# Two-trunk encoder: neighbourhood-attention probabilities of six heads turned by VectorE and DRAM instead of TensorE

## The chip, the core and the metric

The kernel runs on one core of a Trainium2 chip. The metric is device time in microseconds (us), the median of several runs of the whole program. The core has a matmul engine (TensorE, PE in the profile, with its weight loads as PEld), VectorE (DVE), ScalarE (ACT), GpSimd (POOL), and SyncE (SP), which here only issues transfers. Each engine works through its own instructions in order, and waits on semaphores for the others. Transfers go through queues of SP, ACT and GpSimd to 16 DMA engines that all share. Matmul results land in PSUM; everything else lives in SBUF.

## The reference

Two inputs, a prompt of 1024 tokens and a sample of 512, go through one encoder layer of width 1024, all in fp32:

```python
xn = rmsnorm(x);  z = xn @ w_in          # q,k,v of A; q,k,v of B; gate A; gate B
o_a = grouped-query attention(qa, ka, va)           # branch A, 8 heads of 64
o_b = neighbourhood attention(qb, kb, vb, rpb)      # branch B, 8 heads of 64
x = x + (sigmoid(ga) * (o_a @ w_proj_a) + sigmoid(gb) * (o_b @ w_proj_b)) @ w_out
x = x + relu(rmsnorm(x) @ w_mlp_up) ** 2 @ w_mlp_down;  y = rmsnorm(x)
```

In branch B the tokens form a grid 64 wide. A query sees a window of 8 rows by 16 columns around it; a learned bias per head is added to each score, everything outside the window is masked, and softmax and the product with the values follow.

## The kernel before

The short trunk (512 tokens, names with `s0`) runs first, then the long one (1024 tokens, `NB = 2`, names with `s1`), then both MLPs. A product of fp32 matrices is three reduced-precision matmuls, high·high, high·low and low·high (`mm3`, lines 195 to 197). So every operand is kept as a high part, which ScalarE makes by a copy that rounds (`ACTIVATE`), and a low part, which VectorE makes by subtracting (`TENSOR_TENSOR`).

The change is in branch B of the long trunk, 797 to 1067 us of the profiled span. Its work is 32 units: 8 heads, and for each four strips of 16 grid columns (j = 1, 2, 0, 3). A strip has 256 queries in two halves of 128, and each half sees 12 rows of 32 columns, 384 keys. One unit is three steps, each a function:

- `s_unit`: two score matmuls 128x384 a half (`sbs`, line 971: the queries hold both parts, the keys come as high and as low part) into one of two PSUM buffers; GpSimd adds bias and mask (`bms`, 957); VectorE's custom reduction adds them to the scores, negates and takes the minimum (974); ScalarE's Exp with its sum (`pbs`, 979); VectorE's reciprocal (981); GpSimd's scaling (982).
- `t_unit`: the probabilities have queries on the partitions, but the value product needs keys there. TensorE transposes six 128x128 pieces (`ptbs`, 994) into PSUM; ScalarE copies the high part, VectorE subtracts the low part (`bhs`, 999 and 1000).
- `v_unit`: four matmuls with the values as the stationary operand (`obs`, 1013). Keys that both halves share are one matmul of 512 columns (2 parts x 2 halves x 128 queries), the others one of 256. `finish_o` adds the two partition halves (`ot_Bs`, `os_Bs`, 439 to 452) and stores the result to DRAM (`obds`, 453) by ACT's queue.

A unit's transposes are written one unit behind its scores and its value product one more (`LS = LV = 1`). Between the steps a filler (`Fill.pull`) puts pieces of other work: 129 steps of the gate projection, three matmuls each (`gpss`), whose tanh is stored by ACT's queue (`zgs`, 430). Every eighth unit brings the query and key projection of the next two heads (`pqbs`, `pkbs`, 96 matmuls); over the last eight units the filler is the output projection of branch A (`proj_a`, `ppas`). The tile scheduler sets the final order on each engine: it may move an instruction against the program's text unless it is marked by `keep_in_program_order`, and nothing on TensorE is marked here. It also inserts the semaphores.

SP's queue loads weights (`raw_..`), bias rectangles (`rects`) and the values in the strips' layout (`vss`, 878; 16 transfers a head). GpSimd's queue carries only the mask and eight key copies here.

## Time and profile before

| | |
|---|---|
| median of 3 runs | 2143.84 us (2143.38 to 2143.88) |
| the profiled execution | 2144.47 us |
| its span in the trace | 2142.7 us |
| granted TensorE clock | 0.999 |
| TensorE, VectorE, ScalarE, GpSimd busy | 99%, 68%, 53%, 17% of the span |
| DMA, mean | 165 GB/s |
| long branch B | 797 to 1067 us: TensorE busy 268.4 of 270.0 us |

The trace's names leave out buffer numbers: `sbs1_0_1` in the program is `sbs` there. In the program, `sbs1_2_1` is the long trunk's head 2, strip 1. A timeline row gives start, length, engine, line and operation, the tile written and the tiles read, and how many instructions of a kind follow each other; in square brackets stands the idle time ahead and what ended it. A group row gives the instructions of one line and shape with total busy time and mean ns of one. A waits row gives the total, the number and the longest of the waits of one line for another. A row with a queue and a kind gives packets, MB and the share of 16 engines' time; a transfer row the median us from issue to landing. `SPq`, `ACTq` and `POOLq` are the issues on a queue.

### The profile page before, as it was taken

What the parts mean: (1) busy time and instruction counts of PE and PEld (TensorE: products, weight loads), DVE (VectorE), ACT (ScalarE), POOL (GpSimd) and SP (SyncE); (2) the same over time, 40 slices, a digit from 0 to 9 for tenths busy, and PEclk for the clock granted to TensorE, in tenths of its full rate; (3) what the DMA queues carried; (4) which work ended last, traced back from release to release, by engine and by line L of the source; (5) the groups of instructions that cost most, each with busy time, mean ns of one, the idle gap of its engine ahead of it and who ended that gap; (6) DMA issues with size and microseconds to landing.
All of it is one profiled execution on the core that took longest, in us unless ns stands there. A gap on an engine that the chain in (4) does not pass through costs nothing.

```text
span 2142.7 us, 32089 instructions
## 1 busy us (share of the span) xinstructions
PE 2115.4 (99%) x10967; PEld 1846.9 (86%) x10967; DVE 1462.8 (68%) x2793; ACT 1145.3 (53%) x2511; POOL 356.1 (17%) x446
## 2 busy tenths in 40 slices
PE   9999999999999999999999999999999999999998
PEld 8888778888897888887888899999999988888887
DVE  6665786767657755556882877778777777759563
ACT  6664653767566644555530566566555643434352
POOL 2232310323232223333200200003000000000000
PEclk9999999999999999999999999999999999999999
DMA  6437557520122133433472665578545799688561
GB/s 191 133 99 208 157 162 249 186 71 25 56 78 69 42 95 108 132 117 111 142 234 105 212 198 182 174 243 208 161 145 155 256 353 342 213 275 280 174 201 64
DMA packets 321259, 354.08 MB, mean 165 GB/s; under 512 B 31551, under 2 KB 255431, under 8 KB 321095
## 3 DMA queue, kind: packets, MB, share of 16 engines
q1 hardware_dynamic: 278647, 280.96, 42.0%
q10 hardware_dynamic: 35296, 50.88, 6.8%
q0 software_dynamic: 7152, 20.19, 3.5%
q8 instruction: 87, 1.43, 0.3%
q14 instruction: 77, 0.63, 0.1%
HBM read 264.85 MB, written 87.88 MB: 165 GB/s over the span
## 4 chain that ended last, share of the span: by engine, by line
PE 68%; issue 1%; DVE 1%; DMA 0%; ACT 0%; SPq 0%; POOL 0%; POOLq 0%; ACTq 0%; DVEq 0%
PE dn L196 7%; PE dn L197 7%; PE dn L195 7%; PE ua L195 2%; PE ua L197 2%; PE ua L196 2%; PE ud L195 2%; PE ud L197 2%; PE ud L196 2%; PE uc L195 2%; PE uc L197 2%; PE uc L196 2%; PE gpss L195 2%; PE gpss L197 2%; PE gpss L196 2%; PE ops L197 1%
## 5 line engine op out<-in xcount | busy, mean ns | idle before, releaser
L197 PE MATMUL dn<-wd,al 128*128 128x512 f32 x624 | 242.8, 389 | 0.0
L196 PE MATMUL dn<-wd,ah 128*128 128x512 f32 x624 | 242.8, 389 | 0.0
L195 PE MATMUL dn<-wd,ah 128*128 128x512 f32 x624 | 242.7, 389 | 0.0
L1273 ACT ACTIVATE ah<-ar 128x512 fp32r<-128x512 f32 x168 | 104.2, 627 | 202.6 <-PE dn L196 190.4
L1274 DVE TENSOR_TENSOR al<-ar,ah 128x512 fp32r<-128x512 f32 x168 | 114.0, 686 | 75.3 <-ACT ah L1273 67.2
L195 PEld LDWEIGHTS dn<-wd,ah 128*128 128x128 f32 x624 | 117.2, 188 | 24.5
L197 PEld LDWEIGHTS dn<-wd,al 128*128 128x128 f32 x624 | 117.2, 188 | 24.2
L196 PEld LDWEIGHTS dn<-wd,ah 128*128 128x128 f32 x624 | 117.2, 188 | 24.2
L749 POOL TENSOR_SCALAR ps<-ps,rls 128x1024 f32<-128x1024 f32 (+1 forms) x96 | 96.8, 1009 | 225.7 <-DVE rls L748 200.3
L788 ACT ACTIVATE pths<-pTs 128x512 fp32r<-128x512 f32 x160 | 94.0, 597 | 74.0 <-PE pTs L783 71.8
L789 DVE TENSOR_TENSOR ptls<-pTs,pths 128x512 fp32r<-128x512 f32 x160 | 107.5, 686 | 37.7 <-ACT pths L788 36.7
L743 DVE TENSOR_REDUCE nms<-ss 128x1 f32<-128x1024 f32 (+1 forms) x96 | 99.8, 1040 | 25.6 <-PE ss L741 25.1
L195 PE MATMUL gpss<-xs_0h,w_gs 128*128 128x512 f32 x256 | 105.6, 412 | 0.5 <-DVE ot_Bs L440 0.4
L746 ACT ACTIVATE ps<-ss,nms 128x1024 f32<-128x1024 f32 (+1 forms) x96 | 93.1, 971 | 22.8 <-DVE nms L743 20.1
L783 PEld LDWEIGHTS pTs<-ident,ps 128*128 128x128 f32 x640 | 78.0, 140 | 28.5 <-POOL ps L749 4.3
L180 POOL TENSOR_TENSOR rs_f<-ms_f,mhalf 128x1 f32<-128x1 f32 x6 | 4.0, 667 | 590.7 <-DVE ms_f L176 590.7
L197 PE MATMUL gpss<-xs_0h,w_gs 128*128 128x512 f32 x256 | 101.1, 395 | 0.3 <-DVE w_gs L190 0.3
L196 PE MATMUL gpss<-xs_0l,w_gs 128*128 128x512 f32 x256 | 101.0, 394 | 0.0
L783 PE MATMUL pTs<-ident,ps 128*128 128x128 f32 x640 | 99.0, 274 | 1.3 <-DVE ptls L789 0.6
L1273 ACT ACTIVATE A<-S 128x512 fp32r<-128x512 f32 x128 | 75.9, 623 | 31.2 <-DVE S L1336 22.4
L957 POOL TENSOR_TENSOR bms<-rects,msks 128x384 f32<-128x384 f32 (+1 forms) x72 | 70.1, 976 | 128.7 <-DVE nmbs L974 107.8
L1392 ACT ACTIVATE c<-c 128x384 f32<-128x384 f32 x96 | 50.3, 524 | 69.6 <-DVE c L1391 69.5
(330 smaller groups left out, 6418.7 us busy)
## 6 DMA issues: line engine op xcount, KB each, us to landing
ar<-ud SPq DMA_DIRECT2D x120, 512.0 KB, 5.2
br<-in_w_mlp_down_dram SPq DMA_DIRECT2D x72, 512.0 KB, 5.4
rawu<-in_w_mlp_up_dram SPq DMA_DIRECT2D x64, 512.0 KB, 4.1
ud<-c ACTq DMA_DIRECT2D x128, 192.0 KB, 3.3
raw_gs<-in_w_in_dram SPq DMA_DIRECT2D x32, 512.0 KB, 4.0
zgs<-sgs ACTq DMA_DIRECT2D x48, 256.0 KB, 2.2
ud<-cs SPq DMA_DIRECT2D x64, 192.0 KB
raw_os<-in_w_out_dram SPq DMA_DIRECT2D x16, 512.0 KB, 3.8
```

What stands on the lines that cost most here:

```text
L195: nc.tensor.matmul(out, ah, bh, start=start, stop=False, **kw)
L196: nc.tensor.matmul(out, ah, bl, start=False, stop=False, **kw)
L197: nc.tensor.matmul(out, al, bh, start=False, stop=stop, **kw)
L743: nc.vector.tensor_reduce(nm_, s, axis=AX.X, op=ALU.max, negate=True)
L746: nc.scalar.activation(p, s, AF.Exp, bias=nm_, accum_out=l)
L749: nc.gpsimd.tensor_scalar(p, p, rl, 1.0, op0=ALU.mult, op1=ALU.mult)
L783: nc.tensor.transpose(pt[:, j * P : (j + 1) * P], PP[u, j][:, kc * P : (kc + 1) * P], ident)
L788: nc.scalar.activation(hi, pt, AF.Copy)
L789: nc.vector.tensor_tensor(lo, pt, hi.bitcast(F32), op=ALU.subtract)
L957: nc.gpsimd.tensor_tensor(bm.rearrange("p (r c) -> p r c", c=32), rects[h][:, ir : ir + kr_n, jr : jr + 32], msk[:, hf * 3 + ct, :].rearra ...
L1273: nc.scalar.activation(hi, src, AF.Copy)
L1274: nc.vector.tensor_tensor(lo, src, hi.bitcast(F32), op=ALU.subtract)
```

## The change

It concerns the long trunk's branch B only. For the 24 units of the first six heads (`moved`):

- Both halves' probabilities lie in one tile of 128x768 (two buffers), written by Exp in an order of 32-wide blocks. VectorE transposes each 32x32 block in place, one instruction of 128x768 (`turn`), written between the next unit's two reductions and its Exps. GpSimd's queue stores the tile to DRAM (`tbs`, 393 KB), and four transfers on SP's queue fetch it back with the blocks placed as a whole transpose needs them (`fetch_t`; 32 partitions, four runs of 768 bytes each). ScalarE copies the high part from SBUF, VectorE subtracts the low part in place, both 128x768.
- The split comes three units behind the scores, the value product four. The value product is six matmuls of 256 columns, since the two halves' keys no longer lie side by side.
- The last eight units keep TensorE's transposes, one and two units behind.

For the whole of the long branch B, TensorE's instructions are marked to keep program order (`held_pe`), the four score matmuls of a unit stand ahead of its two reductions, the gate and output stores go by SP's queue (`store[0]`), and the values of heads 1 to 6 are loaded strip by strip instead of head by head. The filler's pulls become 5 or 6 with a mean of 5.33 instead of 5.67, what is left of the gate projection is drained ahead of the 25th unit's split, and `proj_a` begins one unit earlier.

```diff
+    held_pe = []
+    def mul(out, a, b, **kw):
+        op = nc.tensor.matmul(out, a, b, **kw)
+        if held_pe:
+            tc.keep_in_program_order(op)
...
-                    nc.scalar.dma_start(dst[c * P : (c + 1) * P, tb * 512 : tb * 512 + 512], sg)
+                    store[0].dma_start(dst[c * P : (c + 1) * P, tb * 512 : tb * 512 + 512], sg)
...
-            nc.scalar.dma_start(dst, b[:, :n])
+            store[0].dma_start(dst, b[:, :n])
...
+            moved = set(units[: n - 8]) if NB == 2 else set()
...
+                if before is not None:
+                    before()
+                pm = ph.tile([P, halves * nkey], F32, tag="pb", name=f"pb{N}_{h}_{j}", bufs=4 // halves)
+                if u in moved:
+                    pm = pm.rearrange("p (b f k i) -> p b f k i", b=4, f=halves, i=32)
...
+            def turn(u):
+                h, j = u
+                pm = PT[u]
+                blocks = pm.rearrange("p b f k i -> p (b f k) i")
+                tc.keep_in_program_order(nc.vector.transpose(blocks, blocks))
+                PT[u] = dram.tile([P, 4, halves * nkc * 32], F32, name=f"tb{N}_{h}_{j}")
+                nc.gpsimd.dma_start(PT[u], pm.rearrange("p b f k i -> p b (f k i)"))
+
+            def fetch_t(u):
+                h, j = u
+                hl = ph.tile([P, 2, 4, halves, nkc, 32], F32R, tag="bh", name=f"bh{N}_{h}_{j}", bufs=3)
+                turned = PT[u].rearrange("(a i) b w -> b i a w", i=32)
+                for b in range(4):
+                    nc.sync.dma_start(
+                        hl[b * 32 : b * 32 + 32, 1].rearrange("p a f k i -> p a (f k i)").bitcast(F32), turned[b]
+                    )
+                PT[u] = hl
...
+                if u in moved:
+                    hi, lo = (PT[u][:, i].rearrange("p a f k i -> p (a f k i)") for i in range(2))
+                    nc.scalar.activation(hi, lo.bitcast(F32), AF.Copy)
+                    nc.vector.tensor_tensor(lo, lo.bitcast(F32), hi.bitcast(F32), op=ALU.subtract)
+                    return
...
+                if u in moved:
+                    seq = [(k + hf, hf, hf + 1) for hf in range(2) for k in range(nkc)]
...
-            LS, LV = (1, 1) if NB == 2 else (2, 1)
+            if moved:
+                store[0] = nc.sync
+                held_pe.append(1)
+            for i, u in enumerate(units):
+                ls = 3 if u in moved else 3 - NB
+                due_t.setdefault(i + ls, []).append(u)
+                due_v.setdefault(i + ls + 1, []).append(u)
...
-                    f = (5 if i < LS else 2 + i % 2) if NB == 1 else 5 + (i % 3 > 0)
+                    f = (5 if i < 2 else 2 + i % 2) if NB == 1 else 5 + (i % 3 == 0)
...
+                if 0 < i <= n and units[i - 1] in moved:
+                    fetch_t(units[i - 1])
```

Over the program TensorE has 144 transposes fewer, 48 value products of 512 columns fewer and 96 of 256 more. VectorE has 24 block transposes and 24 subtracts from SBUF more and 48 from PSUM fewer; GpSimd's queue has 24 stores more, SP's 96 fetches and the 40 stores that leave ACT's. Three places of the order matter. The first is TensorE at the head of the branch (`pkbs` is the first head pair's key projection, `sbs1_0_1` the first unit's scores); before:

```order
L195 MATMUL pkbs1_0_1_9339<-xs1_1h1_4943,w_bks1_0_9224 128x512
L196 MATMUL pkbs1_0_1_9339<-xs1_1l1_4945,w_bks1_0_9224 128x512
L197 MATMUL pkbs1_0_1_9339<-xs1_1h1_4943,w_bks1_0_9224 128x512
L195 MATMUL gpss1_3328_0_0_9420<-xs1_0h0_4501,w_gs1_3328_0_9230 128x512
L196 MATMUL gpss1_3328_0_0_9420<-xs1_0l0_4503,w_gs1_3328_0_9230 128x512
L197 MATMUL gpss1_3328_0_0_9420<-xs1_0h0_4501,w_gs1_3328_0_9230 128x512
L195 MATMUL gpss1_3328_0_0_9420<-xs1_0h0_4501,w_gs1_3328_0_9230 128x512
L196 MATMUL gpss1_3328_0_0_9420<-xs1_0l0_4503,w_gs1_3328_0_9230 128x512
L197 MATMUL gpss1_3328_0_0_9420<-xs1_0h0_4501,w_gs1_3328_0_9230 128x512
L971 MATMUL sbs1_0_1_9371<-kBs1_0_0_9235,qBs1_0_9234 128x384
L195 MATMUL gpss1_3328_0_0_9420<-xs1_0h0_4501,w_gs1_3328_0_9230 128x512
```

The same place of the change (every matmul now has the line of `mul`, 197):

```order
L197 MATMUL pkbs1_0_1_9339<-xs1_1l1_4945,w_bks1_0_9224 128x512
L197 MATMUL pkbs1_0_1_9339<-xs1_1h1_4943,w_bks1_0_9224 128x512
L197 MATMUL sbs1_0_1_9371<-kBs1_0_0_9235,qBs1_0_9234 128x384 x4
L197 MATMUL gpss1_3328_0_0_9402<-xs1_0h0_4501,w_gs1_3328_0_9230 128x512
L197 MATMUL gpss1_3328_0_0_9402<-xs1_0l0_4503,w_gs1_3328_0_9230 128x512
```

The four scores now come straight behind the key projection, ahead of the first gate matmul. The second place is VectorE in the unit whose scores are `sbs1_2_2` (head 2, its second strip); before:

```order
L440 TENSOR_TENSOR ot_Bs1_1_0_10192<-obs1_1_0_10187,ot_Bs1_1_0_10192 64x512
L974 ISA sbss1_2_2_0_10201,nmbs1_2_2_0_10202<-sbs1_2_2_10198,bms1_2_1_0_10104 128x384
L452 TENSOR_TENSOR os_Bs1_1_0_10195<-ot_Bs1_1_0_10192 64x256
L190 TENSOR_TENSOR w_bqs1_2_10053<-raw_bqs1_2_0_10051,w_bqs1_2_10053 128x512
L974 ISA sbss1_2_2_1_10212,nmbs1_2_2_1_10213<-sbs1_2_2_10198,bms1_2_1_1_10117 128x384
L981 RECIPROCAL rlbs1_2_2_0_10207<-lbs1_2_2_0_10205 128x1
L1000 TENSOR_TENSOR bhs1_2_1_10232<-ptbs1_2_1_0_10230,bhs1_2_1_10232 128x3x128
L1000 TENSOR_TENSOR bhs1_2_1_10232<-ptbs1_2_1_1_10231,bhs1_2_1_10232 128x3x128
L981 RECIPROCAL rlbs1_2_2_1_10218<-lbs1_2_2_1_10216 128x1
```

The same unit of the change:

```order
L1002 ISA sbss1_2_2_0_10112,nmbs1_2_2_0_10113<-sbs1_2_2_10107,bms1_2_1_0_10034 128x384
L460 TENSOR_TENSOR os_Bs1_1_1_10099<-ot_Bs1_1_1_10096 64x256
L1002 ISA sbss1_2_2_1_10115,nmbs1_2_2_1_10116<-sbs1_2_2_10107,bms1_2_1_1_10038 128x384
L1046 STREAM_TRANSPOSE pbs1_2_1_10051<-pbs1_2_1_10051 128x768
L1036 RECIPROCAL rlbs1_2_2_0_10124<-lbs1_2_2_0_10122 128x1
L1036 RECIPROCAL rlbs1_2_2_1_10129<-lbs1_2_2_1_10127 128x1
L1067 TENSOR_TENSOR bhs1_1_0_10028<-bhs1_1_0_10028 128x768
L448 TENSOR_TENSOR ot_Bs1_1_2_10170<-obs1_1_2_10163,ot_Bs1_1_2_10170 64x512
```

The two subtracts of the unit before are gone; the transpose of the unit before stands behind the two reductions, and the subtract is that of a unit three back. The third place is SP's queue a little further on, in the change (`bhs` the fetch, `obds` the output store, `zgs` the gate store, `vss` a value strip):

```order
L438 DMA zgs1_1_4662<-sgs1_3328_3_0_10220 128x512
L461 DMA obds1_4664<-os_Bs1_1_0_10248 64x256
L1056 DMA bhs1_2_2_10251<-tbs1_2_2_10197 32x4x192 x4
L900 DMA vss1_2_10064<-vds1_4660 32x4x128 x4
L438 DMA zgs1_1_4662<-sgs1_3328_3_1_10306 128x512
L461 DMA obds1_4664<-os_Bs1_1_3_10319 64x256
L1056 DMA bhs1_2_0_10322<-tbs1_2_0_10272 32x4x192 x4
```

Before, SP's queue held there only loads of weights, bias rectangles and values:

```order
L223 DMA raw_bqs1_2_0_10051<-in_w_in_dram 128x8x128
L223 DMA raw_bks1_2_0_10054<-in_w_in_dram 128x8x128
L872 DMA rects1_3_10130<-biases_97 128x768
L223 DMA raw_gs1_3328_4_0_10174<-in_w_in_dram 128x8x128
L878 DMA vss1_3_10132<-vds1_4660 32x4x128 x16
```

Each unit now has four fetches and an output store in the line of SP's issues, between the loads.

More of the change, by code (lines that the diff above doesn't have):

```diff
@@ L406, in run @@
         fill = Fill()
+        store = [nc.scalar]
         def gate(goff, dst, c0=0, c1=NC8):
@@ L815, in load_o @@
                 t = slot([P, 2, T], F32R, f"oX{N}_{br}_{k}", first and br + k == 0)
-                cut = partial(split, t[:, 0, :], t[:, 1, :], raw[:, :T])
+                cut = partial(split, t[:, 0, :], t[:, 1, :], raw[:, :T], br == 0 and NB == 2)
                 if hold is None:
@@ L863, in run @@
             rects, strips, bms, PT = {}, {}, {}, {}
+            units = [(h, j) for h in range(8) for j in (1, 2, 0, 3)]
+            n = len(units)
+            moved = set(units[: n - 8]) if NB == 2 else set()
             def raw_here(name):
@@ L970, in s_unit @@
                         ]
-                        nc.tensor.matmul(so, qk[h // 2][0][:, h % 2, q0 : q0 + P], kv, start=(i == 0), stop=(i == 1))
+                        mul(so, qk[h // 2][0][:, h % 2, q0 : q0 + P], kv, start=(i == 0), stop=(i == 1))
+                sums = []
+                for hf in range(halves):
+                    nm = f"{N}_{h}_{j}_{hf}"
                     sb = ph.tile([P, nkey], F32, tag="sb", name=f"sbs{nm}", bufs=2)
@@ L1055, in run @@
                     if i % 8 == 7 and qp is not None:
+                        if NB == 2 and i == n - 9:
+                            for _ in range(NC8):
+                                next(qp)
+                            for _ in range(3):
+                                oa_held.pop(0)()
                         for _ in qp:
```

160 lines of the change are left out of this document (111 added, 49 removed).

## The prediction, made before the change ran

> **What bounds the kernel now.** I read the page's engine totals first, then TensorE's waits in the long branch B (797 to 1067 us), then that stretch cut into windows.
>
> ```profile
> PE 2115.4 (99%) x10967; PEld 1846.9 (86%) x10967; DVE 1462.8 (68%) x2793; ACT 1145.3 (53%) x2511; POOL 356.1 (17%) x446
> PE sbs L971 <- DVE kBs L937: 0.8, 1, 0.8
> PE gpss L195 <- DVE bhs L1000: 0.4, 1, 0.4
> PE obs L1013 <- issue: 0.2, 1, 0.2
> core 0: us, PE busy (x) PEld busy (x) DVE busy (x) ACT busy (x) POOL busy (x), PEclk, DMA share, GB/s
> 830.00:865.00 35.00, 34.82 (x162) 28.27 (x161) 16.65 (x46) 13.50 (x27) 7.38 (x10) 1.00 0.28 80
> 865.00:901.00 36.00, 36.00 (x186) 30.14 (x185) 24.17 (x67) 22.10 (x49) 15.98 (x21) 1.00 0.52 154
> ```
>
> TensorE is busy throughout at the full granted clock; in 270 us of branch B it waits three times, 1.4 us in all. So a matmul taken away there is time taken away, and a new wait there is time added. The two windows show two kinds of stretch. 865 to 901 holds six attention units (6.0 us each): VectorE is 67% busy, DMA 52%. 830 to 865 holds mostly the next pair's query and key projection: both are slack. Three six-unit stretches (18 of the 24 moved units) are where the new work must fit; the two units at each projection have room.
>
> **The transposes removed.** A matmul's busy time overlaps its neighbour's, so I price by starts.
>
> ```profile
> 867.92 0.82 PE L994 MATMUL ptbs<-ident,pbs 128*128 128x128 f32 x6
> 868.81 0.39 PE L196 MATMUL gpss<-xs_0l,w_gs 128*128 128x512 f32 x1
> 869.04 0.39 PE L197 MATMUL gpss<-xs_0h,w_gs 128*128 128x512 f32 x1
> 870.66 0.85 PE L1013 MATMUL obs<-bhs,vss 128*128 128x512 f32 x4
> 871.34 0.52 PE L971 MATMUL sbs<-kBs,qBs 128*128 128x384 f32 x2
> 639.76 0.28 PE L195 MATMUL zvs<-wh_vs,xs_1h 128*128 128x256 f32 x1
> 639.88 0.28 PE L196 MATMUL zvs<-wl_vs,xs_1h 128*128 128x256 f32 x1
> ```
>
> Matmuls of 512 columns start 0.23 apart (868.81, 869.04). Six transposes and one such matmul, whose own row is left out, take 867.92 to 868.81, 0.89 us; the transposes cost 0.89 − 0.23 = 0.66 a unit, 0.11 each. 24 × 0.66 = **−15.8 us**.
>
> **The value product.** It is now six matmuls of 256 columns in place of two of 512 and two of 256. Before it takes 870.66 to 871.34, 0.68 us. Matmuls of 256 columns start 0.12 apart in the value projection, each with its own weight load, so 6 × 0.12 = 0.72: +0.04 × 24 = **+1.0**. That its moving operand comes in runs of 32 columns I price at nothing: the scores' keys already come so (a 32-column window of each grid row). 256 columns at half of 512's 0.23 would make it 0.69, so zero is the other bound.
>
> **The head of the branch.** Program order now puts the first unit's four scores straight behind the last key projection; before, six gate matmuls filled that place.
>
> ```profile
> 795.90 0.39 PE L197 MATMUL pkbs<-xs_1h,w_bks 128*128 128x512 f32 x1
> 797.57 0.45 PE L971 MATMUL sbs<-kBs,qBs 128*128 128x384 f32 x1
> 796.32 1.19 ACT L935 ACTIVATE kBs<-pkbs 64x512 fp32r<-64x512 f32 x2 [3.28 <-PE pkbs L197]
> 797.54 1.38 DVE L937 TENSOR_TENSOR kBs<-pkbs,kBs 64x512 fp32r<-64x512 f32 x2 [2.85 <-ACT kBs L935]
> ```
>
> The projection ends at 795.90 + 0.23 = 796.13. The first score needs the high half of the keys (ACT, 797.51) and the second the low half (VectorE, 798.92). With no gate work between, TensorE idles 1.4 and then, behind one score of 0.17, another 1.2: **+2.6**. Zero would need an order that isn't held. The same place for the last pair of heads goes the other way.
>
> ```profile
> 999.43 0.39 PE L197 MATMUL pkbs<-xs_1h,w_bks 128*128 128x512 f32 x1
> 1001.10 0.62 PE L971 MATMUL sbs<-kBs,qBs 128*128 128x384 f32 x2
> 1002.52 0.62 PE L971 MATMUL sbs<-kBs,qBs 128*128 128x384 f32 x2 [0.79 <-DVE kBs L937]
> 1003.20 0.98 PE L994 MATMUL ptbs<-ident,pbs 128*128 128x128 f32 x6
> 1004.30 0.50 PE L195 MATMUL ppas<-oXs,w_pas 128*128 128x512 f32 x1
> 1001.08 1.38 DVE L937 TENSOR_TENSOR kBs<-pkbs,kBs 64x512 fp32r<-64x512 f32 x2 [1.49 <-ACT kBs L935]
> ```
>
> Before, two scores (0.35) fill 1.42 us and six transposes (0.66) fill 1.10: 1.5 lost. Now six gate matmuls and six value matmuls (6 × 0.23 + 6 × 0.12 = 2.1 us) stand between projection and scores, so the second score starts at 999.66 + 2.1 + 0.17 = 1001.93 against low keys at 1002.46: 0.5 lost. **−1.0**, between 0 and −1.5.
>
> **What VectorE takes over.** Per moved unit it drops two subtracts from PSUM and gains a block transpose and a subtract of 128x768.
>
> ```profile
> L1000 DVE TENSOR_TENSOR bhs<-ptbs,bhs 128x384 fp32r<-128x384 f32 x44 | 22.6, 549 | 8.0 <-ACT bhs L999 7.9
> L190 DVE TENSOR_TENSOR w_gs<-raw_gs,w_gs 128x512 fp32r<-128x512 f32 x14 | 9.2, 686 | 2.5 <-ACT w_gs L184 2.4
> L190 DVE TENSOR_TENSOR w_bqs<-raw_bqs,w_bqs 128x512 fp32r<-128x512 f32 x6 | 5.5, 930 | 2.1 <-ACT w_bqs L184 2.1
> 873.59 1.40 DVE L190 TENSOR_TENSOR w_bqs<-raw_bqs,w_bqs 128x512 fp32r<-128x512 f32 x1
> 873.41 1.03 POOL L957 TENSOR_TENSOR bms<-rects,msks 128x384 f32<-128x384 f32 x1 [4.01 <-DVE nmbs L974]
> 879.82 2.35 POOL L957 TENSOR_TENSOR bms<-rects,msks 128x384 f32<-128x384 f32 x1
> ```
>
> No row shows either operation at 768 columns. 128 columns more cost 0.14 us (0.549 to 0.686), so I estimate 0.96 for 768. Net 2 × 0.96 − 2 × 0.55 = +0.82 a unit. A stretch shrinks from 36.0 by 6 × (0.66 − 0.04) and by the 0.23 of gate work that each unit now leaves for later, to 30.9 us; VectorE goes from 24.17 to 24.17 + 6 × 0.82 = 29.1, 94%. Everything of this is hidden behind TensorE unless VectorE is held up, and it is when it reads two SBUF tiles beside GpSimd: the 1.40 us split beside the 1.03 us mask sum, 0.71 over the ordinary 0.69. The new subtract is of that kind and GpSimd runs four operations a unit. With 0.7 on each of six, VectorE needs 33.3 in 30.9: 2.4 late, 7.2 over three stretches. TensorE feels that at once, since its scores wait in the held order for a score buffer (two) that both reductions free.
>
> **What the DMA queues take over.** A unit stores 393 KB and fetches it back, 0.393 MB each way.
>
> ```profile
> q1 hardware_dynamic: 39380, 28.90, 31.1%
> q0 software_dynamic: 1296, 2.69, 4.3%
> q0 software_dynamic: 7152, 20.19, 3.5%
> kBs<-kBs POOLq DMA_DIRECT2D x8, 256.0 KB, 3.4
> msks<-in_mask_dram POOLq DMA_DIRECT2D x1, 576.0 KB, 7.6
> L979 ACT ACTIVATE pbs<-sbss,nmbs 128x384 f32<-128x384 f32 x64 | 39.3, 615 | 29.9 <-DVE nmbs L974 25.8 <-DVE rlbs L981 1.6 <-POOL bms L957 1.0
> L979 ACT ACTIVATION_READ_ACCUMULATOR pbs<-sbss,nmbs 128x1 f32 x64 | 12.0, 188 | 0.0
> L982 POOL TENSOR_SCALAR pbs<-pbs,rlbs 128x384 f32<-128x384 f32 x64 | 39.7, 625 | 44.5 <-DVE rlbs L981 23.8 <-PE ptbs L994 9.2 <-PE ppas L197 6.7
> ```
>
> In the window 760 to 1075 SP's queue (the first row) takes 0.311 × 315 / 28.90 = 3.39 us of all 16 engines per MB, so a fetch 1.33. GpSimd's queue takes 3.71 per MB over the page (third row) and 5.0 in the window: a store 1.46 to 1.97; I take 1.46, the row with more bytes. A stretch then needs 0.52 × 36 + 6 × 2.8 = 35.5 in 30.9, so DMA ends up to 4.6 late. How late it may be: with two probability buffers, the Exps of unit i+2 wait for the store of unit i. Two units, 10.2 us, must hold one landing and then two Exps with their sums (1.61), a scale (0.63) and the transpose (0.96), 3.2: a store may take 7.0. The nearest rows are 3.4 (256 KB) and 7.6 (576 KB, at the branch's start); from 3.4 the slack is 3.6, so up to 1.0 a stretch leaks, 3.0 in all. At 7.6 a unit would take (7.6 + 3.2) / 2 = 5.4, +0.3 × 18 = 5.4; at the dear store price (0.5 more a store, 7.6 late a stretch) 4.0 leak, 12.0. The projections behind each stretch, at a DMA share of 0.28, empty the queues.
>
> VectorE's lateness and the DMAs' fall on the same TensorE waits, so they aren't added: bounds 0 and 12.0, and I take half of the 7.2, **+3.6**: w_bqs's mean of 0.93 lies a third of the way from 0.69 to 1.40, and DMA adds its share.
>
> The ACT copy is 128x768 in place of two of 384, so nothing is added there; the gate and output stores leave ACT's queue. GpSimd's 24 store issues lie in its idle time, 16 of 36 us being busy.
>
> **The sum.** −15.8 + 1.0 + 2.6 − 1.0 + 3.6 = −9.6 from the profiled execution's 2144.47 gives 2134.9. The runs' median lies 0.6 below that execution: **2134.3 us**. Without the stretch term (−13.2) it is 2130.7; with all of VectorE's lateness (7.2) 2137.9.
>
> **The rivals.** *A, nothing is late.* The collisions miss, and the stores land like the key copies: 2130.7, or 2129.7 with the value product at zero. For it: three waits in 270 us; against it: 94% on VectorE.
>
> *B, VectorE becomes the bound of the stretches.* If every new subtract waits out a whole GpSimd operation (1.03) a stretch needs 29.1 + 6.2 = 35.3 in 30.9, 13.2 late in three, and 2144.47 − 13.2 + 13.2 − 0.6 = 2143.9: no change that can be told. For it: the two rows at 873; against it: w_bqs, in the same stretches, averages 0.93, a third of that wait. [...]
>
> *C, slower: SP's queue.* It issues in order and now carries, in a unit, four fetches, four value loads, the output store and some gate and weight traffic.
>
> ```profile
> 782.94 7.49 SPq L878 DMA_DIRECT2D vss<-vds x16
> obds<-os_Bs ACTq DMA_DIRECT2D x24, 64.0 KB, 1.9
> ```
>
> An issue takes 7.49 / 16 = 0.47, so ten take 4.7 of the 5.1 us. A fetch waits there for its store's landing, and an output store for its sum; if either holds the queue for 1.9 us (an output store's landing) a unit takes 6.6, +1.5 × 18 = 27 against 13.2 gained: 2157. It decides from 13.2 / 18 = 0.73 us a unit. For it: SP is the one queue with no slack; against it: a fetch has about five us in hand before its value product four units on, and not every unit has all ten.
>
> That the change doesn't do what it says is excluded by its instruction order: 144 transposes are gone.
>
> **How the numbers follow.** Forecast 0.57 (2131.5 to 2138.5), A 0.10, B 0.17, C 0.16. No change is within 0.2%, 4.3 us of 2143.84, about what a measurement can tell here. Faster: 0.57 + 0.10 + a quarter of B = 0.71; same: the rest of B, 0.13; slower: C, 0.16. The range 2128 to 2144 leaves out C and the ends of A and B.
>
> **What would show it.** Right: no transposes before the last eight units; TensorE's only new long wait 1.4 and 1.2 us on the keys at the branch's head; a six-unit stretch at 31 to 32 us with VectorE near 90%; value products about 0.72 a unit. A: stretches at 30.9. B: scores waiting for VectorE's reductions all through the stretches, subtracts near 1.9 us. C: value matmuls waiting on the subtract, it on the copy, that on a fetch. I am wrong if a block transpose takes well over 0.96, if the store lands later than 7.0, or if anything outside branch B moves.

## The result: slower by 1.0%, and the profile after

The median of after is 2164.75 us (2162.64 to 2169.93, 4 runs) against 2143.82 (2143.38 to 2143.88) before: a ratio of 1.0102 [1.0084, 1.0119]. The forecast was 2134.3 in a range up to 2144; sign and size are both wrong. The profiled execution of after took 2162.64 us with a span of 2160.9, 18.2 longer than the 2142.7 of before, and that is what is accounted for below.

TensorE's windows come first. The row of before is branch B from 797, just behind its key projection's end, to the first matmul of the next projection (`ppbs`); the last row of after is its six-unit stretch of 865 to 901, as shown of before in the prediction.

```profile
797.00:1067.00 270.00, 268.42 (x1310) 220.76 (x1309) 173.15 (x464) 143.44 (x306) 91.22 (x115) 1.00 0.42 122
```

```profile
core 0: us, PE busy (x) PEld busy (x) DVE busy (x) ACT busy (x) POOL busy (x), PEclk, DMA share, GB/s
797.00:1083.00 286.00, 257.84 (x1217) 215.50 (x1217) 192.68 (x461) 137.69 (x279) 112.01 (x139) 0.96 0.61 180
797.00:933.00 136.00, 134.09 (x640) 113.41 (x639) 92.69 (x227) 68.86 (x141) 64.72 (x84) 1.00 0.66 192
933.00:972.00 39.00, 29.24 (x129) 23.24 (x130) 24.65 (x58) 17.20 (x35) 18.41 (x20) 0.96 0.64 190
972.00:1006.00 34.00, 23.80 (x113) 19.85 (x111) 17.36 (x42) 14.08 (x23) 9.03 (x10) 0.88 0.50 150
1006.00:1083.00 77.00, 70.71 (x338) 58.99 (x339) 57.98 (x137) 37.55 (x81) 19.85 (x26) 0.94 0.56 168
865.00:901.00 36.00, 36.00 (x177) 30.66 (x176) 28.80 (x67) 18.77 (x40) 22.80 (x28) 1.00 0.74 225
```

The branch was to shrink and grew by 16 us in these windows. TensorE's idle time went from 1.6 us (270.00 − 268.42) to 28.2 (286.00 − 257.84). It is not spread out. Up to 933, where the scores of 19 of the 24 moved units lie (16 in before), 1.9 us are idle; the third six-unit stretch loses 9.8 in 39, the place of the last head pair 10.2 in 34, the rest 6.3. A second column tells of a loss the sum had no term for: the granted clock, 1.00 up to 933, is 0.96, 0.88 and 0.94 behind it. TensorE's waits name what it waited for (total, times, longest); of the 11.5 us in the first row, 1.3 belong to the head of the branch:

```profile
PE sbs L197 <- ACT kBs L961: 11.5, 2, 10.2
PE obs L197 <- issue: 5.9, 3, 2.5
PE gpss L197 <- ACT w_gs L184: 3.8, 2, 2.9
PE ppas L197 <- ACT oXs L184: 3.8, 1, 3.8
PE sbs L197 <- DVE kBs L965: 1.7, 2, 1.0
PE obs L197 <- DVE bhs L1084: 1.5, 1, 1.5
```

**The third stretch.** "issue" in the second row names no operation. It is three value products, and the timelines of the third one tell more:

```profile
951.58 0.39 PE L197 MATMUL gpss<-xs_1h,w_gs 128*128 128x512 f32 x1
952.00 0.60 ACT L437 ACTIVATE sgs<-gpss 128x512 f32<-128x512 f32 x1 [0.82 <-PE gpss L197]
952.50 0.83 ACT L1066 ACTIVATE bhs<-bhs 128x768 fp32r<-128x768 f32 x1
953.36 0.96 DVE L1067 TENSOR_TENSOR bhs<-bhs 128x768 fp32r<-128x768 f32 x1 [1.93 <-ACT bhs L1066]
954.42 0.95 PE L197 MATMUL obs<-bhs,vss 128*128 128x256 f32 x6 [2.46 <-issue]
```

Read it backwards. The value product (954.42) starts 0.1 after the subtract ends (954.32). The subtract starts when the high copy ends. The copy stands on ACT behind a gate's tanh, and the tanh waits for the last gate matmul (951.58), which in TensorE's held order is the last work ahead of this value product. So TensorE stands still for a tanh, a copy and a subtract. The product at 946.86 waits in the same way, on a copy behind two Exps and a tanh, and these Exps had waited for scores that TensorE runs only behind the value product before. At 939.99 the copy (937.27) stands behind two Exps and a weight split, and the first Exp had waited for a store of the probabilities to land, since it writes into that store's buffer:

```profile
935.06 0.62 ACT L1024 ACTIVATE pbs<-sbss,nmbs 128x384 f32<-128x384 f32 x1 [1.65 <-DMA tbs<-pbs]
ACT pbs L1024 <- DMA tbs<-pbs: 19.7, 8, 6.9
```

The second row is the branch's total. Of its 19.7 us, 18.0 lie before 933, where no value product waits. The copies themselves aren't late for want of their data: over the branch they wait 2.0 us in all for a fetch. Counted on ACT, the copies of the 15th to the 19th unit stand behind the Exps of the unit four on; of the 14 before them only the 11th does, the others stand behind those of the unit three or two on.

The three products are 5.9 of the 9.8 us. Another 2.9, from 956.1, are a gate weight's split (ACT, 957.89): SP had issued its load at 941.65, but the split stands on ACT behind an Exp, and that waits for the scores of 955.22.

**The last head pair.** The 10.2 us wait, from ACT, TensorE and SP's queue, each in order of time:

```profile
995.83 0.59 ACT L447 ACTIVATE ot_Bs<-obs 64x512 f32<-64x512 f32 x1 [8.19 <-PE obs L197]
...
997.58 1.99 ACT L184 ACTIVATE oXs<-rawos 128x1024 fp32r<-128x1024 f32 x2
999.59 0.59 ACT L937 ACTIVATE qBs<-pqbs 64x512 fp32r<-64x512 f32 x1
1003.05 1.06 ACT L184 ACTIVATE oXs<-rawos 128x1024 fp32r<-128x1024 f32 x1 [2.87 <-DMA rawos<-oads]
...
1004.75 1.19 ACT L961 ACTIVATE kBs<-pkbs 64x512 fp32r<-64x512 f32 x2
994.90 0.89 PE L197 MATMUL obs<-bhs,vss 128*128 128x256 f32 x6
1005.99 0.69 PE L197 MATMUL sbs<-kBs,qBs 128*128 128x384 f32 x1 [10.20 <-ACT kBs L961]
999.19 0.32 SPq L822 DMA_DIRECT2D rawos<-oads  x1
```

ACT has nothing to do from 987.6 to 995.8: its next instruction is the sum of a value product that the held order puts behind the whole key projection. Behind that sum stand the splits of the next projection's first operands, one of which waits for a load that SP issues only at 999.19, and behind them the keys. That load doesn't wait for a store: SP waits 7.6 us for a buffer that the split of the first weight frees (`w_pas`, ACT, 997.06), and this split stands behind the same sum. The change has a hand in this order. The section on it names TensorE's marks alone, but it also marks these splits, and the last pair's query and key copies for the second 512 tokens, to keep program order, and the first weight's load on SP. In before the three splits stood at 992.82, and behind them ACT waited for the projection's own results alone.

**The clock.** Two one-microsecond windows behind the long wait, and three longer ones ahead of and behind the wait of 2.9 us (the column behind the five engines is the granted clock):

```profile
1010.00:1011.00 1.00, 1.00 (x4) 0.81 (x3) 0.98 (x3) 1.00 (x5) 0.00 (x0) 0.50 0.80 160
1012.00:1013.00 1.00, 1.00 (x7) 0.81 (x6) 0.63 (x1) 0.04 (x1) 1.00 (x2) 1.00 0.75 301
...
953.70:957.12 3.42, 1.66 (x10) 1.37 (x10) 1.70 (x3) 0.59 (x1) 0.00 (x0) 1.00 0.98 283
957.12:960.53 3.41, 1.21 (x4) 0.73 (x5) 3.41 (x9) 2.99 (x6) 3.20 (x4) 1.00 0.36 122
960.53:963.95 3.42, 3.42 (x10) 2.67 (x9) 1.00 (x3) 0.00 (x0) 2.02 (x2) 0.50 0.79 214
```

TensorE stops at 995.8; at 998.1 its clock is halved, and it is whole again at 1011.7, after 5.7 us of work. Four matmuls run in the window at 1010, seven in that at 1012. A wait of 2.9 us from 956.1, behind three of 1.7 to 2.5, was enough for 3.4 us of half clock up to 964; the 3.8 us wait at 1015 cost another 3.4. Busy time times (1 − clock) over these stretches gives 1.7, 2.5 and 1.5: 5.7 us.

The clock changes at 960.53, 963.95, 998.08, 1011.74, 1018.56 and 1021.98. The steps between are 1, 10, 4, 2 and 1 times 3.41 us, so in this run the clock changes on a grid of 3.41 us and not at a fixed time after a stop. What followed a step of the grid goes with how long TensorE was busy in it: 1.66 us ahead of 957.12, and it kept its clock; 1.21 ahead of 960.53, 1.12 ahead of 998.08 and none ahead of 1018.56, and it lost half. It came back behind 3.42, 3.41 and 3.19 us (963.95, 1011.74, 1021.98) and not behind 1.60 (1008.32). 0.50 and 1.00 are the only levels here, and a step in which TensorE worked for a third of the time (1.21 of 3.41 us) was followed by half the clock.

**The sum.** From the end of the first key projection (796.1 before, 795.3 after) to the first `ppbs` matmul (1066.8 and 1083.0) the branch takes 270.7 and 287.7 us, 17.0 more. Idle time makes 27.9 of it: the 26.6 of the tables and the head's first wait, 1.3, which ends at 796.8, ahead of the tables' first window. The slow clock adds 5.7. So the work at full clock is 16.6 less (the prediction had −14.8, transposes and value product). After reaches the branch 0.8 us earlier than before; in e12 to e14 below that point moves by 1.3 us from run to run. Behind the branch nothing moves from the first `ppbs` matmul to TensorE's last (1068.14 and 1068.18), but from there to the span's end it is 7.77 us before and 9.74 after. The difference lies in a closing drain of GpSimd, which the program's end waits for. Its longest, in before and in after (ns, least/median/most):

```profile
L1795 POOLq DRAIN  x3: 46/102/5166, 2136.7 to 2142.4; - x3
L1918 POOLq DRAIN  x3: 46/102/7127, 2152.9 to 2160.6; - x3
```

### The profile page after: what moved, and what is told of

Same layout as the page of the kernel before. It is cut to its first block, busy times and chain, and to the rows that moved or that the text cites. A ratio compares the mean times of both kernels' runs of the same rounds, so it can differ in the third digit from the quotient of the medians.

```text
span 2160.9 us, 32004 instructions
## 1 busy us (share of the span) xinstructions
PE 2104.1 (97%) x10871; PEld 1841.4 (85%) x10871; DVE 1484.3 (69%) x2793; ACT 1140.5 (53%) x2487; POOL 377.0 (17%) x470
## 4 chain that ended last, share of the span: by engine, by line
PE 66%; DVE 1%; DMA 1%; issue 1%; ACT 1%; POOL 0%; SPq 0%; POOLq 0%; ACTq 0%; DVEq 0%
PE dn L197 20%; PE ua L197 6%; PE ud L197 6%; PE uc L197 6%; PE gpss L197 5%; PE ops L197 4%; PE ub L197 3%; PE ppbs L197 2%; PE pkbs L197 2%; PE pqbs L197 2%; PE ppas L197 2%; PE dnf L197 2%; PE pTs L791 1%; PE obs L197 1%; PE sbs L197 1%
## 5 line engine op out<-in xcount | busy, mean ns | idle before, releaser
L197 PE MATMUL dn<-wd,ah 128*128 128x512 f32 x1248 | 384.3, 389 | 0.0
L197 PE MATMUL gpss<-xs_0h,w_gs 128*128 128x512 f32 x512 | 189.3, 405 | 5.1 <-ACT w_gs L184 3.8
L197 PE MATMUL ud<-B,A 128*128 128x384 f32 x768 | 143.7, 335 | 0.7 <-DVE c L1514 0.7
L197 PE MATMUL uc<-B,A 128*128 128x384 f32 x768 | 143.7, 334 | 0.0
L197 PE MATMUL ua<-B,A 128*128 128x384 f32 x768 | 138.8, 334 | 0.0
L757 POOL TENSOR_SCALAR ps<-ps,rls 128x1024 f32<-128x1024 f32 (+1 forms) x96 | 96.9, 1010 | 225.5 <-DVE rls L756 200.2
L197 PEld LDWEIGHTS ud<-B,A 128*128 128x128 f32 x768 | 134.0, 188 | 1.1 <-DVE c L1514 1.1
L197 PEld LDWEIGHTS uc<-B,A 128*128 128x128 f32 x768 | 134.1, 188 | 0.2 <-ACT A L1396 0.2
L197 PEld LDWEIGHTS ua<-B,A 128*128 128x128 f32 x768 | 133.7, 188 | 0.2
L197 PE MATMUL ops<-wh_os,mgs 128*128 128x512 f32 x384 | 119.5, 391 | 0.0
L197 PEld LDWEIGHTS gpss<-xs_0h,w_gs 128*128 128x128 f32 x512 | 96.8, 190 | 24.6 <-ACT w_gs L184 4.5
```

The source lines that it names most:

```text
L197: op = nc.tensor.matmul(out, a, b, **kw)
L757: nc.gpsimd.tensor_scalar(p, p, rl, 1.0, op0=ALU.mult, op1=ALU.mult)
```

## The experiments

Every ratio is against before on the same chip. Compare with 1.0102 for the change.

**e1, e2, e3, e4: is it an order on ACT, or TensorE's?** My first theory named ACT's order. e1 takes the three splits from between the query and key projection of the last pair and puts them behind it:

```diff
@@ the projections' loop
                                 next(qp)
-                            for _ in range(3):
-                                oa_held.pop(0)()
                         for _ in qp:
                             pass
+                        if NB == 2 and i == n - 9:
+                            for _ in range(3):
+                                oa_held.pop(0)()
```

> The three input splits of branch A's output projection are written behind the last head pair's query and key split instead of ahead of it; nothing else changes. Theory (two separate delays on ScalarE's queue; this is the second: the last pair's key copies stand behind splits whose loads are late): TensorE's wait of 10.2 us ahead of the 25th unit's scores falls to 0.5 to 1.5 us, the granted clock stays at 1.00 after it (about 3.6 us of slowed work), the three value product waits of the third stretch (1.7, 1.7, 2.5) stay: about 2151 us (2147 to 2156). Rival (SP's queue and its transfers are the limit, the splits only show it): the wait moves to the first matmuls of the output projection and the time stays at 2160 to 2166.

Measured: 2170.18, 1.0122 [1.0102, 1.0142]: nothing gained. The last pair's wait on the high keys is gone (the head's 1.3 us is left), and the next row took its place:

```profile
PE ppas L197 <- ACT oXs L184: 15.2, 3, 10.2
```

The wait moved as the rival had it, though the time lies above its range too, and this run doesn't show that SP's queue is the reason. TensorE's held order needs the splits' products a little later, and they were as late as before.

e2 keeps ACT's tanh, Exps, high copies and output sums in the program's order:

```diff
+    def act(*a, **kw):
+        op = nc.scalar.activation(*a, **kw)
+        if held_pe:
+            tc.keep_in_program_order(op)
+
-                    nc.scalar.activation(sg, g_, AF.Tanh, scale=0.5)
+                    act(sg, g_, AF.Tanh, scale=0.5)
...
-                    nc.scalar.activation(hi, lo.bitcast(F32), AF.Copy)
+                    act(hi, lo.bitcast(F32), AF.Copy)
```

> ScalarE's Exps, tanhs, high copies and output copies of the long branch B keep program order, so the high copy of a unit stands behind the Exps of the unit three later, not four; nothing else changes. Theory (first delay: the order that the scheduler gave ScalarE puts the high copies a unit late in the third stretch): the value product waits of 1.7, 1.7 and 2.5 us and the lowered clock at 960 vanish, the 10.2 us wait for the last pair's keys stays: about 2156 us (2151 to 2160). Rival (the fetched probabilities land late): ScalarE then waits for the fetch instead, the value products wait as before, 2162 to 2168.

Measured: 2171.89, 1.013 [1.011, 1.015]. The high copies stood one unit earlier than in the change, as e2 meant them to, and it was slower than either range: the value products still waited, 10.4 us in two. e3 is e1 and e2 together.

> Both edits: ScalarE's order held and the splits behind the keys. Theory (both delays are ScalarE's order and add up, with the slowed clock that follows each): 2132 to 2142 us, against a sum without any new wait but that at the branch's head of 2130.7. Rival (SP's queue or DMA is the limit of the third stretch): 2148 to 2155, with waits on fetches.

Measured: 2169.4, 1.0114 [1.0097, 1.0131], far above both ranges. From TensorE's and ACT's waits in e3:

```profile
PE obs L197 <- issue: 12.5, 2, 7.3
ACT w_gs L184 <- DMA raw_gs<-in_w_in_dram: 20.4, 3, 9.6
```

With its order held, ACT blocks on a weight split whose load is late (20.4 us in three waits); the product waits only moved. The theory that ACT's order alone is the cause fell: something upstream is late, and any fixed order stands still for it.

e4 leaves TensorE's order to the scheduler (`held_pe.append(1)` becomes `pass`).

> TensorE's order is not held (the scheduler orders it), all else as in the change. Rival theory (the held order of TensorE is what costs): 2130 to 2145 us and no wait above 2 us in branch B. Theory (ScalarE's order costs, whoever orders TensorE): the last pair's keys are as late, TensorE may fill a part of the 10 us with other work: 2148 to 2165.

Measured: 2163.84, 1.0093 [1.0072, 1.0113], the same as the change. Holding TensorE's order, by itself, isn't the cause either. (In e14 below, with less moved, releasing it does gain.)

**e6 and e7: which part of the change?** e6 leaves the move out; all units keep TensorE's transposes. Since the strip loads hang on `moved`, the values are loaded head by head again too.

```diff
-            moved = set(units[: n - 8]) if NB == 2 else set()
+            moved = set()
...
-            if moved:
+            if NB == 2:
                 store[0] = nc.sync
                 held_pe.append(1)
```

> Everything of the change but the move itself: no unit is moved, TensorE transposes all 32 again (one and two units behind), with TensorE's order held, four scores ahead of both reductions, the new filler counts and the early output projection, and the gate and output stores on SP's queue. Theory (the move costs, since its fetches crowd SP's queue with the weight loads and output stores): 2143 to 2150 us, the 10 us wait for the last pair's keys gone or below 3 us. Rival (held order and the early splits cost, whatever moves): 2155 to 2168, with the same waits as in the change from 1000 us on.

Measured: 2150.1, 1.0029 [1.0018, 1.0040]. The surroundings (held order, stores on SP's queue, early output projection) cost 5.9 us, of which the two key waits at the head are 2.3. The move with its strip loads, in these surroundings, costs the other 15.0 of 20.9. From TensorE's last matmul to the end it is 7.73: the late end belongs to the move.

e7 takes one line out, so that gate and output stores stay on ACT's queue:

```diff
             if moved:
-                store[0] = nc.sync
                 held_pe.append(1)
```

> The gate and output stores stay on ScalarE's queue, as before the change; all else as in the change. Theory (SP issues in order, and each output store holds it until a value product four units back has run, up to 9.9 us; fetches, weight and value loads behind it come late, and ScalarE's order with them): the waits of the third stretch and of the last pair's keys shrink from 17 us in all to below 6, 2136 to 2148 us. Rival (the fetch's wait for its own store, or DMA's bandwidth, is what makes loads late): 2158 to 2168, with SP's longest waits on the store of the probabilities.

Measured: 2154.56, 1.0047 [1.0032, 1.0062], by the medians 10.2 less than the change: between the two ranges. SP's queue in the change, and then in e7 (what its issues wait for):

```profile
SPq L461 <- DVE os_Bs L460: 28.8, 8, 9.9
SPq L461 <- DVE nmbs L1002: 19.1, 8, 7.3
SPq L438 <- ACT sgs L437: 10.5, 6, 5.1
```

```profile
SPq L1056 <- DMA tbs<-pbs: 38.4, 12, 5.3
SPq L1056 <- DMA obds<-os_Bs: 19.2, 6, 6.4
```

In the change 58 us of SP's time go to waiting, in order, for sums and tanhs whose stores stand in its line; in before they weren't there. In e7 it waits for what the fetches themselves need (the stores of probabilities), or, as the profile infers it, for an output store's landing. TensorE is busy 33.78 of the 39 us of 933 to 972 where it was 29.24. One caution: without these stores the scheduler also orders ACT otherwise there (of the copies that stood one unit late, only the 17th to the 19th still do, the 17th between two Exps), so e7 shows what the stores on SP cost and not which of the two carries it. The wait on the last pair's keys stays: 10.6 us.

**e8 to e11: the last pair and ACT's order, with the stores on ACT.** e8 is e7 with e1's edit.

> As the run before, and the three splits of the output projection written behind the last pair's keys. Theory (SP's queue late, and the splits ahead of the keys a second cost): 2132 to 2142 us. Rival (splits and keys are one delay, which only moves from the keys to the output projection, as in the first run): within 3 us of the run before.

Measured: 2156.06, 1.0055 [1.0039, 1.0072]; again the wait moves to the next projection (10.3 us there). e9 instead begins branch A's projection three units earlier and no longer pins its first load's place:

```diff
-                w["w_proj_a"][0], 0, P, f"pa{N}_0", slot_left, NB == 2, oa_held if NB == 2 else None, raw_of
+                w["w_proj_a"][0], 0, P, f"pa{N}_0", slot_left, False, oa_held if NB == 2 else None, raw_of
...
-                if NB == 2 and i == n - 9:
+                if NB == 2 and i == n - 12:
                     pa = proj_a(ph, raw_here)
                     next(pa)
+                if NB == 2 and i == n - 9:
                     f = 2
```

> Stores on ScalarE's queue, and branch A's output projection begun three units earlier (21st unit instead of 24th) with its first weight load free to move, so that its inputs are loaded and split before the last pair's keys; all else as in the change. Theory (the 10.6 us wait for the last pair's keys is ScalarE's: it stands idle for a value product while the splits, and the keys behind them, are queued after it, and the loads of those splits are late on SP): the wait falls below 3 us, the clock stays at 1.00 after it; from 2154.6 about 2143 (2139 to 2147). Rival (the wait only moves to the output projection's inputs, as when the keys were put first): 2152 to 2158.

Measured: 2151.06, 1.0032 [1.0021, 1.0044], between the two ranges. Two of TensorE's waits:

```profile
PE ppas L197 <- ACT w_pas L184: 4.8, 1, 4.8
PE obs L197 <- DVE bhs L1067: 2.8, 1, 2.8
```

The second is a value product in the third stretch, taken up at e11. The 10 us wait is gone; by the medians 3.5 us come out as time against e7, and 4.8 come back as a wait at the projection.

e10 holds ACT's order as e2 does, on e9.

> As the run before, with ScalarE's Exps, tanhs, high copies and output copies of the long branch B in program order. Theory (with the stores off SP the weight loads come in time, and holding the high copies at three units behind the scores removes the waits of 3.2 and 2.5 us in the third stretch): 2134 to 2141 us. Rival (weight splits then block ScalarE as when the order was held with the stores on SP; the loads, not the place of the stores, are late): 2148 to 2160 with ScalarE's longest wait on a weight load.

Measured: 2156.63, 1.0056 [1.0041, 1.0071], 5.6 worse than e9: in the rival's range, though ACT's longest wait there, 6.3 us, is for a store of the probabilities and its one wait for a weight's load is 3.5. e11 holds one thing alone: a unit's Exps are issued behind the high copy of the unit four back.

```diff
+            def exp_behind(u, *a, **kw):
+                four_back = units.index(u) - 4
+                if four_back >= 0 and units[four_back] in hi_op:
+                    with tc.issue_after(hi_op[units[four_back]].ins):
+                        return nc.scalar.activation(*a, **kw)
+                return nc.scalar.activation(*a, **kw)
...
-                        nc.scalar.activation(
+                        exp_behind(
+                            u,
...
-                    nc.scalar.activation(hi, lo.bitcast(F32), AF.Copy)
+                    hi_op[u] = nc.scalar.activation(hi, lo.bitcast(F32), AF.Copy)
```

> As the run with stores on ScalarE's queue and the output projection begun early, and one constraint more: a unit's high copy stands on ScalarE ahead of the Exps of the unit four later (nothing else of ScalarE is held). Theory (in the third stretch the high copy stands behind Exps that wait for a store of the probabilities, and the value product behind it): the waits of 3.2 us ahead of the 17th unit's value product and the slowed clock there go; from 2151.1 to 2146 (2144 to 2149). Rival (the wait is the fetch's or VectorE's): 2150 to 2153.

Measured: 2147.36, 1.0012 [1.0003, 1.0022], by the medians 3.7 less than e9. In the third stretch:

```profile
933.00:972.00 39.00, 35.52 (x170) 29.46 (x169) 26.40 (x60) 18.52 (x40) 19.94 (x26) 1.00 0.75 228
```

e9 has 32.80 there at a clock of 0.96. Its 2.8 us wait shows what the edit takes away:

```profile
945.65 0.61 ACT L1024 ACTIVATE pbs<-sbss,nmbs 128x384 f32<-128x384 f32 x1 [3.27 <-DMA tbs<-pbs]
946.27 0.82 ACT L1066 ACTIVATE bhs<-bhs 128x768 fp32r<-128x768 f32 x1
948.14 1.00 PE L197 MATMUL obs<-bhs,vss 128*128 128x256 f32 x6 [2.78 <-DVE bhs L1067]
```

The Exp waits 3.27 us for a store of the probabilities, and the copy stands behind it. In e11 no copy stands behind the Exps of the unit four on. So the place of the high copies on ACT is one cause, and the stores' landing is what it exposes; holding the whole of ACT was the wrong tool for it. It still isn't faster than before: the waits at the head and at the last pair are left.

**e12 to e14: less moved, and the head filled.** e12 moves 16 units (two head pairs) instead of 24, on e9, and pulls four steps of the gate projection ahead of the first scores. These two edits weren't told apart.

```diff
-            moved = set(units[: n - 8]) if NB == 2 else set()
+            moved = set(units[:16]) if NB == 2 else set()
...
                 held_pe.append(1)
+                fill.pull(4)
```

> Only the first four heads' 16 units are moved (the third stretch and the last pair keep TensorE's transposes, in held order), stores on ScalarE's queue, output projection begun early, and 12 gate matmuls ahead of the first scores. Theory (in the first two stretches the move gains its 0.62 us a unit whole, what costs lies after them, and the head's 2.7 us is the lack of other work): 16 x 0.62 = 9.9 off, the program's end 2.0 later, 1 to 4 for the held order behind: 2137 to 2141 us, faster than before; no wait above 0.5 us at the head. Rival (the held order costs as much as the move gains): 2143 to 2149.

Measured: 2137.95, 0.9969 [0.9957, 0.9981]: faster than before by 0.3%. The window 797 to 933, where the scores of its moved units lie:

```profile
797.00:933.00 136.00, 136.00 (x657) 116.03 (x656) 94.93 (x230) 71.63 (x145) 64.96 (x83) 1.00 0.66 197
```

Nothing is idle, with DMA at 0.66: where the queues and ACT's order allow it, the move is hidden. e13 sends e12's probabilities by SP's queue instead of GpSimd's (`nc.gpsimd.dma_start(PT[u], ...)` becomes `nc.sync.dma_start`).

> As the run before, with the probabilities stored by SP's queue instead of GpSimd's. Theory (the program's end is 2.0 us longer in every run that stores them by GpSimd's queue, and only there, because of those stores): the end, from TensorE's last matmul to the span's end, falls from 9.7 to 7.8 us, and the time by up to 2 us if SP's queue bears the stores: 2135 to 2141. Rival (the end is longer for another reason): it stays at 9.7, and SP, waiting for each block transpose, makes the fetches later: 2140 to 2150.

Measured: 2143.88, 0.9994 [0.9985, 1.0004]. The time from TensorE's last matmul to the span's end falls from 9.29 to 7.74, so the late end does come from stores on GpSimd's queue. But TensorE is idle 5.5 us more in the branch (11.9 against 6.4), and its clock is 0.96 between 933 and 972; the gain at the end is lost in the branch. SP now waits over 19 us for the transposes and reciprocals ahead of these stores; that TensorE's new waits come from there isn't shown.

e14 is e12, and TensorE's order is released after the 20th unit (`held_pe.clear()` at `i == 19`), since e12's remaining waits lay behind the moved units.

> As the run with four heads moved (stores on ScalarE's queue, output projection early, gate work ahead of the first scores), with TensorE's order held only up to the 20th unit, the last that has a moved value product. Theory (behind the moved units the held order is what waits: 6.4 us idle between 933 and 1001): those waits fall to 1 to 3 us, 2132 to 2136 us. Rival (the waits there come from ScalarE's and SP's order, whoever orders TensorE, as in the run with TensorE free throughout): 2136 to 2142.

Measured: 2134.55, 0.9954 [0.9938, 0.9971], the best of these: 9.9 us below before. All that TensorE still waits for in the branch:

```profile
PE obs L197 <- DVE bhs L1084: 2.7, 2, 1.5
PE gpss L197 <- DVE ot_Bs L448: 0.9, 1, 0.9
PE obs L197 <- DVE ot_Bs L448: 0.4, 1, 0.4
```

So moved transposes are worth about what was priced: 16 × 0.62 = 9.9 on paper. That the two are equal is partly chance, since e14 also has other surroundings, and e12, from which it comes, an end that is 1.5 us later than before's.

## Why the prediction was wrong, step by step

**Right: the prices of the work.** Groups and transfers of after:

```profile
L1067 DVE TENSOR_TENSOR bhs<-bhs 128x768 fp32r<-128x768 f32 x22 | 23.2, 1053 | 6.2 <-ACT bhs L1066 5.6 <-DMA obds<-os_Bs 0.6
L1046 DVE STREAM_TRANSPOSE pbs<-pbs 128x768 f32<-128x768 f32 x23 | 22.2, 966 | 0.0
tbs<-pbs POOLq DMA_DIRECT2D x24, 384.0 KB, 3.5
```

The block transpose takes 0.966 us (0.96 estimated), the store lands after 3.5 in the median (3.4 to 7.6 considered, 7.0 allowed). A value product takes 0.73 (0.72). The six units from 858.9 take 30.6 us (30.9), and VectorE is 80% busy between 865 and 901 (near 90% forecast). The head's two gaps, by starts as the prediction counts them, are 1.4 and 1.2 us, as forecast. From the projection's end to the 17th unit's scores it is 137.0 us before and 126.6 after: 10.4 gained in spite of the head. In that stretch TensorE runs 90 transposes and six gate matmuls less; at 0.11 and 0.23 they give 11.3, less the head's 2.7 it is 8.6. So a transpose was worth a little more than its price.

**Right: rival B did not come.** The new subtract averages 1.053, not 1.9; VectorE isn't the bound, though GpSimd's scaling went from 0.625 to 0.781 beside it. No subtract waited out a whole GpSimd operation (1.03), as the rival had every one do: the 24 take 0.928 to 1.369 us, 17 of them under 0.96.

**Wrong: "VectorE's lateness and the DMAs'", +3.6.** This term asked whether engines and queues have enough time in a stretch. For TensorE the first two stretches lost nothing, so there it was too high. Its DMA half did happen on ACT: a store lands in 3.5 us where 7.0 were allowed, and yet the Exps wait 19.7 us for stores. The sum gave a store two whole units, but a unit's block transpose, and so its store, stands behind the next unit's reductions (the 17th unit's store is issued at 931.07, and the 19th's Exp waits for it until 935.06). The third stretch lost 9.8 us of idle time and 1.7 of slow clock, from an order: high copies and a weight split behind Exps and a tanh that wait for a store, or for matmuls that TensorE runs late itself. Busy shares, which the term was made from, can't show this; the order of ACT in the changed program, against TensorE's held order, could have. e11, which changes that order alone, takes the stretch's idle time from e9's 6.2 us to 3.5.

**Wrong: "the last pair of heads goes the other way", −1.0.** I moved the second score against the low keys' time of before, 1002.46, as if the keys stayed where they were. The step looked at TensorE's order alone. On ACT the sum of a late value product and the splits stand ahead of the keys, in an order that the change itself marks. It cost 10.2, then 3.8 at `ppas`, and 4.0 of slow clock behind both. e1 and e8 show that the keys' place isn't the cause (the wait moves on); e9 shows that starting the operands earlier and unpinned is what takes it away.

**Wrong: "the gate and output stores leave ACT's queue", costed at nothing.** No gain on ACT shows, and SP lost. Issue times were counted for SP (rival C's 4.7 of 5.1 us), but these stores' waits are 58 us of its queue. e7 prices it, together with the order on ACT that changes with it: 10.2 us.

**Rival C had the nearest time (2157) and half the mechanism.** SP's queue held by output stores is what its rows show, up to 9.9 us at a time where the rival had 1.9. But its chain, value product on subtract on copy on fetch, breaks at the last link: the copies waited 2.0 us in all for fetches. And it was priced per unit over 18 units, while the loss sits in one stretch and one head switch. Its chance of 0.16 was too low: the row against it, five us in hand for a fetch, spoke of fetches alone, and the queue also carries stores that wait for their sums.

**Wrong: no step for the clock** (5.7 us), **and the end** (2.0 us): "if anything outside branch B moves" was listed as a sign of being wrong, and it was one. The end is GpSimd's closing drain, 5.17 us before and 7.13 after.

**Open.** Why the scheduler puts the high copies one unit later in the third stretch than in the first two; which share of e7's 10.2 us is SP's queue and which the order on ACT that changes with it; and which of e12's two edits gives how much. After's own runs spread over 7.3 us, those of before over 0.5; the cause wasn't tried. One candidate, not shown, is where the clock's grid lies against the program: e7, with the same two waits at the head, has a clock of 0.99 over 797 to 933, after one of 1.00.

## What to carry to other kernels

Price an instruction that moves to an in-order queue by what it will wait for there (58 us on SP's queue here) and by what stands behind it, not by its issue time. Where one engine's order is held, walk the other engines' orders against it at every switch of stage: each operand made behind something that itself needs that engine is idle time, and no busy share shows it. An edit that moves one wait usually finds the next late operand, so look for what made the operand late; and moving less of the work, where the queues have room, was worth more here than mending every wait.

## What the runs showed of the hardware that was not expected

- In after TensorE's clock changes on a grid of 3.41 us. From 797 us to the last matmul it was halved behind the steps in which TensorE was busy 35%, 33% and 0% of the time, and behind none of 49% or more; it came back behind 94% and 100%, and not behind 47% and 0%. A wait of 2.9 us sufficed in after, and one of 3.1 us cost nothing in e9 (`pkbs`, between 972 and 1001, where the clock is 1.00). In after three slow stretches cost 5.7 us beside the waits themselves.
- In these runs stores on GpSimd's queue in mid-program lengthen the program's end: GpSimd's closing drain takes 5.17 us without them (before, e6, e13), 6.47 with 16 (e12, e14) and 7.13 with 24 (after), 0.082 us for each store of probabilities. What GpSimd does in it isn't shown.
